# The last projection of a hybrid decoder block as seven half-size products for each pair of token tiles

## The chip, the core and the metric

The kernel runs on one core of a Trainium2 chip. The metric is the time of one execution on the device, in microseconds. The core has five engines that run side by side, each with its own queue of instructions, and meet by semaphores: TensorE (PE in the profile; its weight loads are PEld), VectorE (DVE), ScalarE (ACT), GpSimd (POOL) and SyncE (SP). SP mostly issues DMA transfers; POOL and ACT issue some too. TensorE writes its products to PSUM, eight banks of 128 x 512 float32. Everything else works in SBUF, 128 partitions wide.

## The reference

`x` holds 1024 tokens of 1024 channels. They are normalised and projected, and run through two token mixers (a dilated attention and a gated delta rule), whose outputs `o_a` and `o_b` are gated. The change touches only what comes after:

```python
y_a = (o_a * silu(dsa_z)) @ w_up_a          # 512 -> 1024
y_b = (o_b * silu(gdn_z)) @ w_up_b
merged = sigmoid(gate_a) * y_a + sigmoid(gate_b) * y_b
x = x + merged @ w_out                      # 1024 -> 1024
return rmsnorm(x, final_norm_w)
```

## The kernel before

**Precision.** Float32 products are made of float16 halves. Each operand is held as a high half (a cast, on ScalarE) and a low half (what the cast lost, one `scalar_tensor_tensor` on VectorE, line 76 by way of `STT`). `mm3_steps` (lines 169 to 179) makes three matmuls for each tile of 128 inner channels: high by high, high by low, low by high.

**Order.** TensorE's order is written out by hand: matmuls run in the order in which the program issues them. For the other engines a scheduler orders the instructions when the program is built, by priority (earlier in the program goes first, `tc.high_priority()` ahead of that) and by when it reckons them to be ready. On the chip each engine then runs its list strictly in order. `in_turn` (line 147) keeps an instruction behind the last matmul issued so far in that order, without a semaphore.

**The feed.** `Feed` (line 198) holds the projections as units of 28 or 32 steps, three matmuls of 512 columns each step, and loads and splits the next unit's weights while one runs. `feed.later(n, fn)` calls `fn` after n more steps. Many units are already made as seven products in place of eight (`seven_products`, line 347): their two-by-two blocks are added and subtracted beforehand, so that seven block products give all four blocks of the result.

**The last units.** Units `gate` 0 to 7 give the tanh of the merge gates, spilled to DRAM (`gsp`). Units `up` 0 to 3 (lines 1453 to 1483) each take two tiles (`dt`) of 128 channels. For each half of the tokens (`hf`, 512) they make the product of branch a in a bank `S` and that of branch b in a bank `mm`. VectorE multiplies each by its gate tile (`sig`, reloaded from DRAM), adds the two to `m` in float32, and ScalarE and VectorE split `m` into `m16`, two resident tiles of 1024 x 1024 float16 in the room of the input `h`. In the same units the output weights are loaded by POOL in eight pieces and split into `wo16`, one 128x1024 cast and one 128x1024 low half each.

**The last product.** Lines 1658 to 1687 go through eight token tiles of 128. For each half of the output columns, 8 channel tiles by 3 matmuls accumulate in a bank `mm`; VectorE adds the bank to `x`, ScalarE squares and sums it. Then come the root, the reciprocal, the scaling by `final_norm_w` and the store. The last tile cuts its second half in 384 and 128 columns, so that less is left after the last matmul. Tiles for gates, x and squares come from one ring of eight (`ring`, line 1640).

Of the kernel before, what the change touches and what calls it, by code (L numbers as in the profile page):

```python
# [10 lines left out]
F32 = mybir.dt.float32  # L11
F16 = mybir.dt.float16
# [8 lines left out]
KT = 8  # L21
# [43 lines left out]
PG_LAG = 20  # L65
PAIR_TICKS = 4
# [4 lines left out]
def hybrid_block(ctx: ExitStack, tc: tile.TileContext, A):  # L71
# [1338 lines left out]
    late, m16, wo16 = [], [], []  # L1410
# [17 lines left out]
    def z_now(br, ct, hf, p, rest):  # L1428
        ts = slice(hf * 512, hf * 512 + 512)
        gate = late[0].tile([128, 512], F32, name="zs", tag="zs", bufs=ZS)  # L1430
        z_silu(gate, p, rest)
        oa = late[0].tile([128, 512], F32, name="oa", tag="oa", bufs=2)
        nc.sync.dma_start(out=oa, in_=oa_d[ct, :, ts])
        STT(gate, gate, H_SCALE, oa, ALU.mult, ALU.mult)
        if (br, ct) not in osp:
            osp[br, ct] = late[1].tile([128, 2, S], F16, name=f"os{br}{ct}")
        n = osp[br, ct]
        SC.copy(n[:, 0, ts], gate)
        TT(n[:, 1, ts], gate, n[:, 0, ts], ALU.subtract)
# [12 lines left out]

    def up_unit(u):
        def gen(w):
            wh, wl = w
            for c in range(2):
                dt = 2 * u + c
                cs = slice(c * 128, c * 128 + 128)
                if c == 0:
                    us = slice(u * 256, u * 256 + 256)  # L1460
                    for n in range(2):
                        with tc.high_priority():
                            st = load_w(A["w_out"][u], n)
                        feed.later(14 + 8 * n, lambda st=st, n=n: (w_hi(st, wo16[0][:, :, us], n), w_lo(st, wo16[0][:, :, us], wo16[1][:, :, us], n)))
                for hf in range(2):
                    ts = slice(hf * 512, hf * 512 + 512)
                    for bi, br in enumerate("ab"):
                        p = bank("S", 2) if bi == 0 else bank("mm", 3)
                        for i, _ in enumerate(mm3_steps(
# [3 lines left out]
                            if i == 3:  # L1473
                                STT(sig[br, dt][:, ts], sig[br, dt][:, ts], 1.0, p, ALU.add, ALU.mult)
                            if i == 3 and bi:
                                m = sig["a", dt][:, ts]
                                TT(m, m, sig["b", dt][:, ts], ALU.add)
                                sc = 0.5 * P_SCALE * H_SCALE
                                SC.activation(m16[0][:, dt, ts], m, AF.Copy, scale=sc)
                                STT(m16[1][:, dt, ts], m, sc, m16[0][:, dt, ts], ALU.mult, ALU.subtract)  # L1480
# [156 lines left out]
    NR = 8  # L1637
    turn = [0]

    def ring(name):  # L1640
        turn[0] += 1
        if turn[0] % 2:
            return kp.tile([128, 16, 64], F32, name=name, tag="kT", bufs=4).rearrange("p a b -> p (a b)")
        return fp2.tile([128, S], F32, name=name, tag="sg2", bufs=4)

    for dt in range(8):
        for br in "ab":
            if len(sig) == NR:
                feed.until(("gate", 7))
            sig[br, dt] = ring(f"sg{br}{dt}")  # L1650
            nc.sync.dma_start(out=sig[br, dt], in_=gsp[br, dt])
    m16.extend(base.tile([128, KT, S], F16, name=f"m{n}", tag=f"h_{n}") for n in ("hi", "lo"))
    wo16.extend(fp2.tile([128, KT, D], F16, name=f"wo{n}") for n in range(2))

    feed.until(("up", 3))
    fw = fp2.tile([128, D], F32, name="fw")
    nc.sync.dma_start(out=fw, in_=A["fnw"])
    for t in range(8):
        tk = slice(t * 128, t * 128 + 128)
        xr = ring("xr")  # L1660
        nc.sync.dma_start(out=xr, in_=A["x"][tk])
        ss = fp2.tile([128, 4], F32, name="ss", tag="ss", bufs=2)
        junk = ring("junk")
        y = ring("y") if t == 7 else xr
        edges = (0, 512, 896, 1024) if t == 7 else (0, 512, 1024)
        for c, (c0, c1) in enumerate(zip(edges, edges[1:])):
            cs = slice(c0, c1)
            p = bank("mm", 3)[:, :c1 - c0]
            mm3(p, (lambda k: m16[0][:, k, tk], lambda k: m16[1][:, k, tk]),
                (lambda k: wo16[0][:, k, cs], lambda k: wo16[1][:, k, cs]))  # L1670
            STT(xr[:, cs], p, P_SCALE, xr[:, cs], ALU.mult, ALU.add)
            SC.activation(junk[:, :c1 - c0], xr[:, cs], AF.Square, accum_out=ss[:, min(c, 1):min(c, 1) + 1])  # L1672
            if c:
                TT(ss[:, 0:1], ss[:, 0:1], ss[:, 1:2], ALU.add)
            if t == 7:
                TT(y[:, cs], xr[:, cs], fw[:, cs], ALU.mult)
        r = ss[:, 3:4]
        SC.activation(ss[:, 2:3], ss[:, 0:1], AF.Sqrt, bias=epsc, scale=1.0 / D)
        V.reciprocal(r, ss[:, 2:3])
        if t < 7:  # L1680
            STT(xr, xr, r, fw, ALU.mult, ALU.mult)
            nc.sync.dma_start(out=A["out"][tk], in_=xr)
        else:
            V.tensor_scalar(y[:, :640], y[:, :640], r, None, op0=ALU.mult)
            nc.sync.dma_start(out=A["out"][tk, :640], in_=y[:, :640])
            SC.activation(y[:, 640:], y[:, 640:], AF.Copy, scale=r)
            nc.scalar.dma_start(out=A["out"][tk, 640:], in_=y[:, 640:])
# [58 lines left out]
def _layout(x, norm_w, w_in, conv_w, a_log, dt_bias, gdn_norm_w, w_up_a, w_up_b, w_out, final_norm_w):  # L1746
# [28 lines left out]
        "w_out": c(unit(np.asarray(w_out)[0])),  # L1775
# [17 lines left out]
```

## Time and profile before

| | |
|---|---|
| median of 3 runs | 1108.44 us (1108.34 to 1109.62) |
| the profiled execution | 1110.44 us, of which the profile's span is 1108.7 us |
| TensorE, VectorE, ScalarE, POOL busy | 96%, 75%, 50%, 5% of the span |
| up units | 936.6 to 1019.5 us of the span |
| last product | 1019.5 to 1102.4 us |
| after the last matmul | 1102.4 to 1108.7 us |

A row of a group reads: line, engine, operation, output<-input, shapes, count, then busy us and mean ns of one, then the idle time of the engine just before these instructions and what ended it. A row of the timeline reads: start, duration, engine, line, operation. A row of the stages gives for each engine its busy time and number of instructions in that stretch, then the granted TensorE clock, the DMA share and GB/s.

### The profile page before, as it was taken

The page shows a single profiled execution, that of the slowest core. Times are in us where ns is not written, and L with a number is a line of the kernel's source. Part 1 is how long each engine was busy: PE and PEld are TensorE (multiplying, and loading weights), DVE is VectorE, ACT ScalarE, POOL GpSimd, SP SyncE. Part 2 cuts the span into 40 slices and gives each one's busy share as a digit, 9 for nine tenths or more (in the row PEclk, how much of TensorE's full clock was granted, in tenths as well). Part 3 has the DMA queues.
Part 4 walks back from the last instruction along what each step waited for, and adds up shares of the span by engine and source line. Part 5 has one row for each costly group of instructions (what it writes and reads, how often), then busy time and mean ns, then how long its engine had stood idle before and what let it go on. Part 6 is the DMA issues. An engine that isn't in the chain of part 4 may idle for free. (4 is left out here: it accounts for less than half of the span.)

```text
span 1108.7 us, 23803 instructions
## 1 busy us (share of the span) xinstructions
PE 1063.1 (96%) x9486; PEld 645.3 (58%) x9486; DVE 829.7 (75%) x1918; ACT 556.1 (50%) x1239; POOL 57.3 (5%) x103
## 2 busy tenths in 40 slices
PE   6999999999999999989999999899999999999997
PEld 5894585775956755756555545445545554444443
DVE  5798997969879679969955997963488777775223
ACT  6455766667666566456635533343454344331211
POOL 1200000000000000000000000000000000110000
PEclk9999999999999999999999999999999999999999
DMA  8135521623516333631235267794785414762221
GB/s 285 62 90 139 135 63 68 168 78 87 140 63 172 88 101 87 156 99 58 69 105 174 69 167 187 219 261 143 232 257 163 144 64 149 250 210 71 76 95 57
DMA packets 102926, 146.88 MB, mean 132 GB/s; under 512 B 31120, under 2 KB 68496, under 8 KB 101920
## 3 DMA queue, kind: packets, MB, share of 16 engines
q1 hardware_dynamic: 79856, 91.49, 28.7%
q0 software_dynamic: 12128, 44.11, 12.7%
q10 hardware_dynamic: 10832, 9.77, 2.7%
q8 instruction: 74, 1.21, 0.5%
q14 instruction: 36, 0.29, 0.1%
HBM read 89.56 MB, written 36.90 MB: 114 GB/s over the span
## 5 line engine op out<-in xcount | busy, mean ns | idle before, releaser
L177 PE MATMUL ps_mm<-h_hi,wlo 128*128 128x512 f16 (+1 forms) x552 | 208.0, 377 | 2.6 <-DVE wlo L76 2.6
L176 PE MATMUL ps_mm<-h_lo,whi 128*128 128x512 f16 (+1 forms) x492 | 185.5, 377 | 2.6 <-issue 1.8
L175 PE MATMUL ps_mm<-h_hi,whi 128*128 128x512 f16 (+1 forms) x492 | 185.7, 377 | 0.0
L177 PEld LDWEIGHTS <-wlo 128*128 128x128 f16 x788 | 77.2, 98 | 92.7 <-issue 3.9
L176 PEld LDWEIGHTS <-whi 128*128 128x128 f16 x848 | 83.1, 98 | 70.9 <-issue 4.8
L175 PEld LDWEIGHTS <-whi 128*128 128x128 f16 x848 | 83.1, 98 | 70.4 <-issue 0.8
L175 PE MATMUL ps_mm<-whi,h_hi 128*128 128x256 f16 x384 | 105.1, 274 | 0.0
L177 PE MATMUL ps_mm<-whi,h_lo 128*128 128x256 f16 x384 | 104.7, 273 | 0.0
L176 PE MATMUL ps_mm<-wlo,h_hi 128*128 128x256 f16 x384 | 104.7, 273 | 0.0
L774 ACT ACTIVATE sm<-sm,osb 128x128 f32<-128x128 f32 (+1 forms) x160 | 69.7, 436 | 56.1 <-DVE osb L770 52.8
L79 DVE TENSOR_TENSOR tl<-ps_G,th 128x256 f16<-128x256 f32 (+1 forms) x96 | 52.1, 542 | 18.6 <-ACT th L789 18.5
L79 DVE TENSOR_TENSOR rt<-rx,tabs 128x512 f32<-128x512 f32 x96 | 64.6, 688 | 1.4 <-ACT rx L580 0.4
L76 DVE SCALAR_TENSOR_TENSOR wlo<-wstage,whi 128x1024 f16<-128x1024 f32 x50 | 61.0, 1222 | 5.7 <-ACT whi L158 5.4
L770 DVE CUSTOM_DVE_ANT_0 sm<-ps_S,amask 128x128 f32<-128x128 f32 (+1 forms) x192 | 59.4, 348 | 7.6 <-PE ps_S L763 7.6
L76 DVE SCALAR_TENSOR_TENSOR ca<-xc,cw,ca 128x512 f32<-128x512 f32 x72 | 53.9, 749 | 9.7 <-ACT ca L997 8.8
L76 DVE SCALAR_TENSOR_TENSOR whi<-wstage,whi 128x512 f16<-128x512 f32 x60 | 40.7, 688 | 20.7 <-ACT whi L322 20.0
L158 ACT ACTIVATE whi<-wstage 128x1024 f16<-128x1024 f32 x49 | 51.6, 1053 | 6.2 <-DMA wstage<-in_w_up 5.2
L784 PE MATMUL ps_G<-cons,sm 128*128 128x128 f32 x280 | 48.3, 276 | 4.8 <-ACT sm L774 2.9
L175 PE MATMUL ps_mm<-wo,mhi 128*128 128x512 f16 (+2 forms) x136 | 49.5, 366 | 0.0
L176 PE MATMUL ps_mm<-wo,mhi 128*128 128x512 f16 (+2 forms) x136 | 49.5, 366 | 0.0
L177 PE MATMUL ps_mm<-wo,mlo 128*128 128x512 f16 (+2 forms) x136 | 49.4, 366 | 0.0
L784 PEld LDWEIGHTS ps_G<-cons,sm 128*128 128x128 f32 x280 | 35.6, 141 | 21.7 <-ACT sm L774 6.5
(335 smaller groups left out, 2538.3 us busy)
## 6 DMA issues: line engine op xcount, KB each, us to landing
wstage<-in_w POOLq DMA_DIRECT2D x68, 512.0 KB, 4.7
og<-osb ACTq DMA_DIRECT2D x32, 132.0 KB, 2.3
og<-og SPq DMA_DIRECT2D x32, 132.0 KB, 2.3
gspa<-gst SPq DMA_DIRECT2D x16, 256.0 KB, 2.2
sga<-gspa SPq DMA_DIRECT2D x8, 512.0 KB, 5.3
wstage<-in_w_up POOLq DMA_DIRECT2D x8, 512.0 KB, 5.2
sgb<-gspb SPq DMA_DIRECT2D x8, 512.0 KB, 5.5
wstage<-in_w_out POOLq DMA_DIRECT2D x8, 512.0 KB, 4.0
```

Source lines behind the costliest of these rows:

```text
L76: (eng or V).scalar_tensor_tensor(out, in0, scalar, in1, op0=op0, op1=op1)
L79: (eng or V).tensor_tensor(out, in0, in1, op)
L158: in_turn(SC.activation(hi[:, 4 * c:4 * c + 4], st, AF.Copy, scale=W_SCALE))
L175: PE.matmul(out, lhsT=wh(k), rhs=mh(k), start=first and i == 0, stop=False, skip_group_check=True)
L176: PE.matmul(out, lhsT=wh(k), rhs=ml(k), start=False, stop=False, skip_group_check=True)
L177: last_pe[0] = PE.matmul(out, lhsT=wl(k), rhs=mh(k), start=False, stop=last and i == len(ks) - 1, skip_group_check=True).ins.name
L770: V.tensor_tensor_reduce(P[:, u, :128 * nk], psc[:, u * 256:u * 256 + 128 * nk], mask, -cexp, -NEG, ALU.add, ALU.min, accum_out=osb[:, 256 ...
L774: SC.activation(P[:, u, :128 * nk], P[:, u, :128 * nk], AF.Exp, bias=osb[:, 256 + hd:257 + hd], scale=-1.0, accum_out=osb[:, 260 + hd:261 ...
L784: PE.transpose(pt[:, c:c + 128], P[:, u, i * 128:i * 128 + 128], ident)
```

## The change

The last product becomes seven products for each pair of token tiles. Take a pair of token tiles (even, odd) as two block rows, the two halves of the 1024 inner channels as x and y, and the weights as four blocks b11, b12, b21, b22 (inner half, output half). With x0, y0 of the even and x1, y1 of the odd tile, the seven left factors are x0, x0+x1, x0+x1+y1, y0, x1+y1, y1 and x0+y0+x1+y1. The right ones are b11, b22-b12, a sum of three blocks, b21, b11-b12, a sum of four, and b22. Each product has four channel tiles in place of eight, with 512 columns.

- `split_wo` loads one group of four 128x512 blocks (one channel tile of each half, by SP into a ring `sgc` of two tiles), makes four sums in float32 and seven splits. It runs four times, from step 14 after the pool is opened (in the last gate unit) and from step 24 of up units 0, 1 and 2. All 14 halves stay resident.
- `m_parts` makes the sums of m and their splits, 256 tokens (two pairs) at a time, for each tile: for the first half of the tokens in the up units at high priority, for the second half in the first pair of the last product.
- The gates are loaded two tiles ahead (`load_sig`); branch b's ring has two tiles.
- In the last product three banks are used for each pair (`G`, `G`, `mm` and `mm` three times in turn). Two bank-to-bank copies on ScalarE carry partial sums. Product 1's bank is subtracted from both halves of the odd tile by VectorE before product 2 is copied into it.
- The last pair ends with the even tile, whose product 6 is cut in 384 and 128 columns.

```diff
+        put(0, b11)
+        in_turn(V.tensor_tensor(b11, b11, b12, ALU.subtract))
+        put(4, b11)
+        TT(b12, b22, b12, ALU.subtract)
+        put(1, b12)
+        put(6, b22)
+        STT(b22, b22, -1.0, b11, ALU.mult, ALU.subtract)
+        put(2, b22)
+        put(3, b21)
+        STT(b21, b22, -1.0, b21, ALU.mult, ALU.subtract)
+        put(5, b21)
+        if kk < 3:
+            load_wo(kk + 1)
...
+        def put(n, y):
+            hi, lo = [m7[hf][n][:, l, kk].rearrange("p (a i) -> p a i", a=2) for l in range(2)]
+            in_turn(SC.activation(hi, y, AF.Copy, scale=M_SCALE))
+            STT(lo, y, M_SCALE, hi, ALU.mult, ALU.subtract)
+
+        if k < 4:
+            put(0, x0)
+            TT(x0, x0, x1, ALU.add)
+            put(1, x0)
+            return
...
+        TT(x0, x0, y1, ALU.add)
+        put(2, x0)
+        put(3, y0)
+        TT(x1, x1, y1, ALU.add)
+        put(4, x1)
+        put(5, y1)
+        TT(y0, y0, x0, ALU.add)
+        put(6, y0)
...
-                if c == 0:
-                    us = slice(u * 256, u * 256 + 256)
-                    for n in range(2):
-                        with tc.high_priority():
-                            st = load_w(A["w_out"][u], n)
-                        feed.later(14 + 8 * n, lambda st=st, n=n: (w_hi(st, wo16[0][:, :, us], n), w_lo(st, wo16[0][:, :, us], wo16[1][:, :, us], n)))
+                load_sig(dt + SIG_AHEAD)
+                if c == 0 and u < 3:
+                    feed.later(WO_LAG, lambda: split_wo(u + 1))
...
-                                STT(sig[br, dt][:, ts], sig[br, dt][:, ts], 1.0, p, ALU.add, ALU.mult)
+                                with tc.high_priority():
+                                    STT(sig[br, dt][:, ts], sig[br, dt][:, ts], 1.0, p, ALU.add, ALU.mult)
...
-                                SC.activation(m16[0][:, dt, ts], m, AF.Copy, scale=sc)
-                                STT(m16[1][:, dt, ts], m, sc, m16[0][:, dt, ts], ALU.mult, ALU.subtract)
+                                if hf == 0:
+                                    with tc.high_priority():
+                                        m_parts(dt, 0)
...
-            mm3(p, (lambda k: m16[0][:, k, tk], lambda k: m16[1][:, k, tk]),
-                (lambda k: wo16[0][:, k, cs], lambda k: wo16[1][:, k, cs]))
...
+        with tc.high_priority():
+            product(0, x, True)
+            SC.copy(y, x)
+            product(1, q, True)
+        if pair == 0:
+            for k in range(4):
+                m_parts(k, 1)
+        with tc.high_priority():
+            for j in (1, 0):
+                rows_[1].add(q, half(j), -1.0)
+            product(2, x)
+            SC.copy(q, x)
+            product(3, y)
+            rows_[0].add(y, half(0))
+            rows_[0].square(half(0))
+        if pair == 0:
+            for k in range(4, 8):
+                m_parts(k, 1)
+        with tc.high_priority():
+            product(4, q)
+            rows_[1].add(q, half(1), -1.0)
+            rows_[1].square(half(1))
+            product(5, x)
+            rows_[1].add(x, half(0), -1.0)
+            rows_[1].square(half(0))
+            rows_[1].finish()
+            if pair < 3:
+                product(6, q)
+                rows_[0].add(q, half(1))
+                rows_[0].square(half(1))
+                rows_[0].finish()
```

`add` is the VectorE addition of a bank to a half of a token tile of x, `square` the sum of squares on ScalarE, `finish` the root, the reciprocal, the scaling of 128x1024 and the store.

More of the change, by code (lines that the diff above doesn't have):

```diff
@@ L1652, in hybrid_block @@
[L1652 to L1653 removed]
+    late.append(fp2)
+    load_wo(0)
+    feed.later(WO_FIRST, lambda: split_wo(0))
+    for dt in range(SIG_AHEAD):
+        load_sig(dt)
+    room = [base.tile([128, KT, S], F16, name=f"m{n}", tag=f"h_{n}").rearrange("p k s -> p (k s)") for n in ("hi", "lo")]
+    m7.append([room[n // 4][:, 2048 * (n % 4):2048 * (n % 4) + 2048].rearrange("p (l k i) -> p l k i", l=2, i=256)
+               for n in range(7)])
```

148 lines of the change are left out of this document (104 added, 44 removed).

## The prediction

> **What bounds the kernel now.** I read the page's head first, then busy time stage by stage, then the matmuls one by one at the seams of the last product.
>
> ```profile
> span 1108.7 us, 23803 instructions
> ...
> PE 1063.1 (96%) x9486; PEld 645.3 (58%) x9486; DVE 829.7 (75%) x1918; ACT 556.1 (50%) x1239; POOL 57.3 (5%) x103
> ```
>
> The page has TensorE busy for 96% of the span; the stages say whether that holds where the change is made.
>
> ```profile
> core 0: us, PE busy (x) PEld busy (x) DVE busy (x) ACT busy (x) POOL busy (x), PEclk, DMA share, GB/s
> 917.20:935.40 18.20, 17.40 (x120) 7.96 (x118) 17.25 (x33) 9.90 (x16) 1.59 (x3) 1.00 0.26 89
> 936.60:1019.50 82.90, 82.90 (x386) 37.60 (x385) 56.36 (x75) 24.09 (x30) 6.36 (x12) 1.00 0.57 194
> 1019.50:1102.40 82.90, 82.90 (x409) 38.85 (x407) 25.47 (x42) 15.29 (x41) 0.00 (x0) 1.00 0.21 76
> 1102.40:1108.70 6.30, 0.20 (x4) 0.02 (x1) 1.57 (x7) 1.47 (x6) 0.00 (x0) 0.87 0.22 83
> ```
>
> The rows are: most of the last gate unit, the four up units, the last product, and the tail after the last matmul. In the up units and the last product TensorE has no gap at all, at a granted clock of 1.00. So matmuls taken out there shorten the span one for one, as long as nothing else becomes late. VectorE is busy for 56.4 of 82.9 us in the up units and 25.5 of 82.9 in the last product: room in the second, little in the first.
>
> ```profile
> 1019.49 0.38 PE L175 MATMUL ps_mm<-wo,mhi 128*128 128x512 f16 x1
> ...
> 1092.01 0.38 PE L175 MATMUL ps_mm<-wo,mhi 128*128 128x512 f16 x1
> ...
> 1096.98 0.38 PE L177 MATMUL ps_mm<-wo,mlo 128*128 128x512 f16 x1
> ...
> 1102.38 0.22 PE L177 MATMUL ps_mm<-wo,mlo 128*128 128x128 f16 x1
> ```
>
> A matmul lasts 0.38 us but the next starts earlier: 1092.01 to 1096.98 are 24 matmuls of one half tile, 23 steps, so 4.97/23 = 0.216 us each. The last product runs from 1019.49 to 1102.4 plus a short drain.
>
> **Matmuls removed.** Before, eight token tiles by two halves by eight channel tiles by three matmuls make 384 matmuls of 512 columns (the last tile's second half is cut in 384 and 128, the same columns). 384 x 0.216 = 82.9, which is the stage. After, four pairs by seven products by four channel tiles by three make 336, with 512 columns again and again one product cut in two. That removes 48 x 0.216 = **10.4 us** of TensorE's time. The other terms ask how much of it is handed back.
>
> **Work added on VectorE before the last product.** Per stage the diff gives: of m, for the first half of the tokens, channel tiles 0 to 3 have two parts and one addition each, tiles 4 to 7 five parts and three additions; 28 parts and 16 additions of 128x256. A part is one ScalarE cast (high half) and one VectorE instruction (low half), so VectorE gets 44 instructions. Of the output weights, four groups of seven parts and four sums make 28 ScalarE casts and 44 VectorE instructions of 128x512. Gone are the 16 m casts and their low halves and the eight weight splits:
>
> ```profile
> L76 DVE SCALAR_TENSOR_TENSOR mlo<-sga,mhi 128x512 f16<-128x512 f32 x16 | 11.1, 692 | 5.6 <-ACT mhi L1479 4.9
> L76 DVE SCALAR_TENSOR_TENSOR xr<-ps_mm,xr 128x512 f32<-128x512 f32 x15 | 10.4, 692 | 44.1 <-PE ps_mm L177 44.1
> L1479 ACT ACTIVATE mhi<-sga 128x512 f16<-128x512 f32 x16 | 10.1, 631 | 47.6 <-DVE sga L79 47.6
> L76 DVE SCALAR_TENSOR_TENSOR wo<-wstage,wo 128x1024 f16<-128x1024 f32 x8 | 9.8, 1224 | 5.7 <-ACT wo L158 5.7
> L76 DVE SCALAR_TENSOR_TENSOR xr<-xr,ss,fw 128x1024 f32<-128x1024 f32 x7 | 9.0, 1285 | 0.2
> L158 ACT ACTIVATE wo<-wstage 128x1024 f16<-128x1024 f32 x8 | 8.4, 1052 | 7.1 <-DMA wstage<-in_w_out 7.0
> ```
>
> What one instruction holds of VectorE lies between two prices, both in the next rows, from the timeline and the groups:
>
> ```profile
> 913.21 4.91 DVE L79 TENSOR_TENSOR ob<-ob,fac 128x512 f32<-128x512 f32 x8
> ...
> 932.84 2.35 DVE L76 SCALAR_TENSOR_TENSOR wlo<-wstage,whi 128x1024 f16<-128x1024 f32 x2
> ```
> ```profile
> L79 DVE TENSOR_TENSOR og<-og,f 128x256 f32<-128x256 f32 x32 | 12.4, 421 | 0.3
> L322 ACT ACTIVATE whi<-wstage 128x512 f16<-128x512 f32 x60 | 37.0, 628 | 14.4 <-DVE wstage L321 8.8 <-PE ps_mm L176 2.9 <-PE ps_mm L177 2.3
> L359 ACT COPY ps_mm<-ps_mm 128x512 f32<-128x512 f32 x30 | 17.2, 573 | 20.2 <-PE ps_mm L177 16.8 <-DMA gspb<-gst 2.0 <-ACT osb L816 0.8
> L1008 ACT ACTIVATE qT<-ca 128x256 f32<-128x256 f32 x8 | 2.9, 411 | 9.9 <-DVE ca L76 9.9
> ```
>
> Eight instructions of 0.69 us in a row take 4.91, so a 128x512 costs (4.91 - 0.69)/7 = 0.60 when the next one is ready; a 128x1024 costs 2.35 - 1.22 = 1.13; 32 of 128x256 took 12.4, 0.39 each. At these prices the up units lose 16 x 0.60 + 8 x 1.13 = 18.6 and gain 44 x 0.60 + 44 x 0.39 = 43.6: 56.4 + 25.0 = **81.4 of 82.9 us**. At full durations they lose 20.9 and gain 44 x 0.69 + 44 x 0.42 = 48.8: 84.3, more than the stage. The trace's rows in a run are the better likeness, since the new work comes in dense bursts, so I take 81.4 and keep 84.3 as the bound. ScalarE goes from 24.1 to 24.1 - 10.1 - 8.4 + 28 x 0.41 + 28 x 0.63 = 34.7 of 82.9 and isn't the bound.
>
> The Trainium skill speaks for the dearer price: in "VectorE: DVE Perf Modes", section Terms, a drain follows every operation and the next cannot issue until the pipe is empty. By that rule the 84.3 would hold; the eight starts 0.60 apart at 0.69 us each disagree, and the row decides.
>
> The second half of the tokens costs the same 44 instructions, 17.2 us, inside the first pair of the last product, and has until the third pair. A pair lasts 84 x 0.216 = 18.1 us; its own VectorE work is six additions at 0.60, two scalings at 1.285 and about 0.6 of small ones, 6.8 us. The third pair reads sums of channel tile 7 from its third product on, at 1019.5 + 36.3 + 5.2 = 1061. From 936.6 to there VectorE has 124.4 us for 81.4 + 17.2 + 13.6 = 112.2: slack 12.2 (7.0 at full durations). What is queued behind a late instruction is everything else on VectorE, the additions that free PSUM banks among them.
>
> **First seam.** Product 0 needs all four weight groups; the last one is due at step 24 of the third up unit, 40 steps of 0.65 us, 26 us, ahead of the end, and has 11 instructions (6.6 us) under evictions that go first. The parts of channel tile 7 come from a sum that stands 4 to 5 us before the up units end, and are read 5.2 + 1.9 us after it. So the cover is about 8 us; each us of VectorE backlog above it is a us of TensorE. With 98% demand I allow **1.5 us** for this and for the seam at the third pair; bounds 0 and 14 (worked out below).
>
> **Handovers inside a pair.** The new copies from bank to bank (row L359, 0.57 us) and each addition (0.69) lie under one product of 12 x 0.216 = 2.6 us before the bank is written again. I cost them at nothing; without the cover it is 0.6 to 1.4 us a handover, and what then waits is the next product.
>
> **Loads.** The weight loads move from POOL's queue to SP's, where the sigmoid tiles, x and the outputs are queued in order too.
>
> ```profile
> sgb<-gspb SPq DMA_DIRECT2D x8, 512.0 KB, 5.5
> wstage<-in_w_out POOLq DMA_DIRECT2D x8, 512.0 KB, 4.0
> xr<-in_x SPq DMA_DIRECT2D x8, 512.0 KB, 3.4
> out<-xr SPq DMA_DIRECT2D x7, 512.0 KB, 2.6
> ```
> ```profile
> 934.32 1.75 SPq L1651 DMA_DIRECT2D sgb<-gspb  x4
> ```
>
> Four loads went out at 934.3, when the memory came free; now two of weights and two of sgb will, as many bytes. The ring of sgb has two tiles: one is freed when the sum of its second half is made, some 2 us into the next channel tile, lands 5.5 later, and is needed 10.4 + 5.2 after that tile's start: cover 8 us, and two more banks after that. In the last product x(t+4) waits for an output to leave: an order of 2.6 + 3.4 us within 18. Nothing, again; a gone cover costs one product, 2.6 us.
>
> **The tail.** Before, the last tile's 384-column piece was 1.3 us ahead of its last matmul and VectorE was free. Now it is 12 short matmuls ahead, 0.7 us, and the scaling of the other tile of the pair (1.285 us) becomes ready at about the same moment.
>
> ```profile
> 1101.29 0.56 DVE L76 SCALAR_TENSOR_TENSOR xr<-ps_mm,xr 128x384 f32<-128x384 f32 x1 [2.48 <-PE ps_mm L177]
> ...
> 1102.67 0.28 DVE L76 SCALAR_TENSOR_TENSOR xr<-ps_mm,xr 128x128 f32<-128x128 f32 x1
> ...
> 1104.20 0.61 ACT L1686 ACTIVATE y<-y,ss 128x384 f32<-128x384 f32 x1 [0.23 <-DVE ss L1679]
> ...
> 1104.78 0.33 SPq L1685 DMA_DIRECT2D out<-y  x1
> ```
>
> The chain from 1102.67 on keeps all its steps. Its first one is late by 0.6 us (the 384 piece still on VectorE) if the scaling comes after it, and by some 2.0 if before. I take **+1.7**, between 0.5 and 2.5.
>
> **The sum.** -10.4 + 1.7 + 1.5 = -7.2 us. The profiled execution took 1110.4 (span 1108.7 and 1.7 around it), 2.0 above the median of the three runs; it would become 1103.2 with a span near 1101.5, and the median 1108.4 - 7.2 = **1101.2**. The forecast's own range, with the tail's bounds and 0 to 4 us of stalls, is 1098.5 to 1104.
>
> **Rivals.**
> (a) *VectorE's backlog reaches TensorE in part*: 5 to 10 us of stall, at the first products of pair 0 or at pair 2. For it: 98% demand. Time 1108.4 - 10.4 + 1.7 + 5 to 10 = 1104.7 to 1109.7; by the middle, about 1107, a small gain or none. Within 0.2% (2.2 us, what a measurement here can tell from no change) is 1106.2 to 1110.7, its upper part.
> (b) *Slower: each low half waits for its high half.* The new work has 84 ScalarE-to-VectorE handoffs up to 1061 (28 of weights, 56 of m).
>
> ```profile
> DVE wo L76 <- ACT wo L158: 5.7, 6, 2.0
> DVE mlo L76 <- ACT mhi L1479: 4.9, 7, 0.7
> ```
>
> The 16 low halves of m waited 4.9 us in all, 0.31 each. If the order written for VectorE leaves each new one that wait, 84 x 0.31 = 26 us, 14 beyond the slack: 1108.4 - 10.4 + 1.7 + 14 = **1114**. It decides from (12.2 + 8.7)/84 = 0.25 us per handoff on. Against it: those waits were made while VectorE had nothing else, and in the last gate unit (first stage row) it reached 17.25 of 18.20 us on work of this kind with 0.8 us of TensorE idle. "TensorE: Matmul & The Clock Gate" of the Trainium skill, section "What's actually happening", adds that an idle window of some 3.4 us halves the clock until work has filled the next one, by which such a stall would cost an estimated 1.7 us more; no gap in these stages is long enough to show it.
> (c) *Nothing is handed back*: the scheduler hides the tail and every stall, 1108.4 - 10.4 + 0.5 = 1098.5 or a little under.
>
> **How the numbers follow.** Forecast 0.62, (a) 0.19, (b) 0.12, (c) 0.07. Faster by over 0.2%: 0.62 + 0.07 + two thirds of (a) = 0.81; within 0.2%: the rest of (a) and a little of (b), 0.07; slower 0.12. The range takes (a) to its middle and most of (c): 1098.2 to 1107.5.
>
> **What would show it.** Right: 48 x 512 columns fewer in the last stage, no TensorE gap over a us from the up units to the last matmul, VectorE over 95% busy in the up units, a tail of 7 to 9 us after the last matmul. Wrong: a TensorE gap just before product 0, 1 or 2 of the first pair that ends with a low half of wo or m (the first seam), or in the third pair (second half of the tokens), or low halves of m and wo that idle VectorE for 0.25 us each (b). An sgb eviction that waits for its load would show the rings too short, which I cost at nothing.

## The result and the profile after

On one chip the kernel before took 1109.03 us (median of 4, 1108.34 to 1111.58) and the changed kernel **1100.66 us** (median of 4, 1098.58 to 1101.08). The ratio is 0.9917, with a 95% interval of 0.9896 to 0.9938. The profiled execution of the changed kernel took 1101.08 us, of which 1099.3 are its span.

The head of the page of the changed kernel:

```profile
span 1099.3 us, 23863 instructions
...
PE 1053.7 (96%) x9426; PEld 640.4 (58%) x9426; DVE 867.3 (79%) x2034; ACT 577.6 (53%) x1307; POOL 53.1 (5%) x95
```

TensorE has 60 matmuls fewer: the 48 removed, and 12 because the half tile that is cut in two pieces is now 12 matmuls made twice where it was 24. VectorE has 116 instructions more and 37.6 us more of busy time. TensorE's share is still 96%, so it is still the bound, of a shorter span. The stages of the changed kernel show where: four rows for the four up units, one for the last product, one for what follows its last matmul (columns as in the stages of before).

```profile
935.50:956.20 20.70, 20.70 (x97) 9.40 (x96) 13.98 (x23) 8.22 (x13) 0.53 (x1) 1.00 0.81 292
956.20:977.00 20.80, 20.80 (x98) 9.46 (x97) 20.80 (x37) 9.32 (x16) 1.59 (x3) 1.00 0.74 245
977.00:997.70 20.70, 20.70 (x98) 9.35 (x97) 20.70 (x39) 9.97 (x19) 0.00 (x0) 1.00 0.54 187
997.70:1018.40 20.70, 20.70 (x98) 9.39 (x97) 20.17 (x43) 6.47 (x16) 0.00 (x0) 1.00 0.33 101
1018.40:1091.90 73.50, 72.68 (x349) 33.52 (x347) 42.91 (x93) 28.01 (x76) 0.00 (x0) 1.00 0.23 79
1091.90:1099.30 7.40, 0.18 (x4) 0.00 (x1) 2.39 (x8) 1.31 (x5) 0.00 (x0) 0.68 0.36 142
```

VectorE is busy for every microsecond of the second and third up unit, and TensorE still has no gap in any of the four. The last product takes 73.5 us where it took 82.9, and all but 0.82 of it is matmuls. Two places are read from the timeline of the changed kernel: the seams at which the last product needs new parts, and the end.

```profile
935.50 0.38 PE L178 MATMUL ps_S<-osa,whi 128*128 128x512 f16 x1
...
943.51 0.69 DVE L79 SCALAR_TENSOR_TENSOR sgb<-sgb,ps_mm 128x512 f32<-128x512 f32 x1 [3.92 <-PE ps_S L180]
...
1016.85 0.42 DVE L79 SCALAR_TENSOR_TENSOR mhi<-sga,mhi 128x256 f16<-128x256 f32 x1
...
1018.38 0.38 PE L178 MATMUL ps_G<-wo0h,mhi 128*128 128x512 f16 x1
...
1025.51 0.38 PE L178 MATMUL ps_G<-wo2h,mhi 128*128 128x512 f16 x1
...
1029.99 1.76 DVE L79 SCALAR_TENSOR_TENSOR mb<-sga,mb 128x256 f16<-128x256 f32 x5
...
1046.21 0.43 DVE L79 SCALAR_TENSOR_TENSOR mb<-sga,mb 128x256 f16<-128x256 f32 x1 [0.30 <-ACT mb L1514]
...
1054.64 0.38 PE L178 MATMUL ps_G<-wo0h,mb 128*128 128x512 f16 x1
...
1090.65 0.54 DVE L79 SCALAR_TENSOR_TENSOR xr<-ps_mm,xr 128x384 f32<-128x384 f32 x1
1091.11 1.27 DVE L79 SCALAR_TENSOR_TENSOR xr<-xr,ss,fw 128x1024 f32<-128x1024 f32 x1
1091.25 0.22 PE L178 MATMUL ps_mm<-wo6h,mb 128*128 128x128 f16 x1 [0.82 <-DVE xr L79]
...
1091.86 0.22 PE L180 MATMUL ps_mm<-wo6h,mb 128*128 128x128 f16 x1
...
1092.84 0.28 DVE L79 SCALAR_TENSOR_TENSOR xr<-ps_mm,xr 128x128 f32<-128x128 f32 x1
...
1094.95 0.33 SPq L1835 DMA_DIRECT2D out<-y  x1
```

Product 2 of a pair is the first that reads parts of channel tiles 4 to 7. At the first seam the parts of tile 7 that products 2 and 3 read are both ready at 1017.27; product 2 starts at 1018.38 + 2 x 2.6 = 1023.6 and comes to tile 7, its fourth, at 1025.51, 8.2 us after they are ready. At the second, the last part for the second half of the tokens is ready at 1046.64, 13 us before product 2 of the third pair starts (1054.64 + 5.2 = 1059.8). The only gap of TensorE is the 0.82 us near the end. There the 128-column piece of the last half tile waits for VectorE, which is still reading the 384-column piece from the same bank; before, the two pieces had banks of their own. After the last matmul VectorE is still at the scaling of the odd tile, and has one product with `fw` besides, ahead of the last addition.

Three stretches, cut at the first up matmul, the first matmul of the last product and the start of the last matmul, give the balance of the profiled executions (936.61, 1019.49 and 1102.38 of a span of 1108.7 before):

| us | up units | last product | after the last matmul's start | sum |
|---|---|---|---|---|
| before | 82.88 | 82.89 | 6.32 | 172.09 |
| after | 82.88 | 73.48 | 7.44 | 163.80 |

So the change is worth **-8.29 us** from the first up matmul on: -10.39 of matmuls (82.89 to 72.50, the last product without a gap, which a run below shows), +0.98 for the gap and the matmuls around it, +1.12 after the last matmul's start.

### The profile page after: what moved, and what is told of

It is laid out like the page before. It is cut to its first block, busy times and chain, and to the rows that moved or that the text cites. A ratio compares the mean times of both kernels' runs of the same rounds, so it can differ in the third digit from the quotient of the medians.

```text
span 1099.3 us, 23863 instructions
## 1 busy us (share of the span) xinstructions
PE 1053.7 (96%) x9426; PEld 640.4 (58%) x9426; DVE 867.3 (79%) x2034; ACT 577.6 (53%) x1307; POOL 53.1 (5%) x95
## 4 chain that ended last, share of the span: by engine, by line
PE 55%; DVE 29%; ACT 7%; DMA 5%; issue 3%; SPq 1%; POOL 0%; ACTq 0%; DVEq 0%; POOLq 0%
PE ps_mm L178 13%; PE ps_mm L180 13%; PE ps_mm L179 13%; DVE rt L82 3%; DVE wlo L79 3%; DVE ca L79 2%; DVE sm L773 2%; ACT sm L777 2%; DVE tl L82 2%; DVE ro L82 2%; DVE pcAl L82 1%; PE ps_S L179 1%; PE ps_S L178 1%; PE ps_S L180 1%; DVE pcBl L82 1%
## 5 line engine op out<-in xcount | busy, mean ns | idle before, releaser
L179 PEld LDWEIGHTS <-h_hi 128*128 128x128 f16 x384 | 45.8, 119 | 1.7
L178 PEld LDWEIGHTS <-h_hi 128*128 128x128 f16 x384 | 45.7, 119 | 1.6
L178 PE MATMUL ps_mm<-h_hi,wlo 128*128 128x512 f16 x120 | 45.6, 380 | 0.8 <-DVE zs L79 0.5
```

The source lines that it names most:

```text
L178: PE.matmul(out, lhsT=wh(k), rhs=mh(k), start=first and i == 0, stop=False, skip_group_check=True)
L179: PE.matmul(out, lhsT=wh(k), rhs=ml(k), start=False, stop=False, skip_group_check=True)
```

## The experiments

All runs are the changed kernel, unedited or with an edit, but for one that edits the kernel before. The medians stand beside the kernel before on the same chip. Sums are those of the table above, made in the same way from each run's trace.

### Does the changed kernel give anything back?

The changed kernel once more, unedited:

> The changed kernel as it is, beside the others on the same chip. Theory: 48 matmuls of 512 columns less (10.4 us), 0.8 us given back in a TensorE gap before the last 128 columns and 1.1 us more between the last matmul and the end: about 8.4 us faster than before, ratio 0.992. Rival: the start of the profiled executions (first matmul 1.0 us earlier after than before) is part of the gain; then about 9.4 us.

1100.9 us against 1109.62, ratio 0.9922 (0.9901 to 0.9943); sum 163.76. A second repetition, in a later comparison on another chip:

> The changed kernel as it is, beside e10_tail on the same chip. Counted from the first matmul of the up units: 163.8 us as before, with 0.8 us of gap before the last piece and 7.4 us after the last matmul.

1100.63 against 1110.04, ratio 0.9923 (0.9904 to 0.9942); sum 163.82. In the three traces of the changed kernel the sum from the first up matmul repeats within 0.06 us, while executions of one kernel spread over some 5 us (1099.02 to 1104.22 in the second of these). The spread comes in ahead of the seam: in all thirteen traces of this document it is 66.4 to 66.5 us from TensorE's 8001st matmul to the first up matmul, but the 8001st itself lies anywhere from 865.8 to 871.5. So an edit is priced by its sum, and its median only says whether it agrees.

The gains of the medians are 8.4, 8.7 and 9.4 us, and their intervals are too wide to tell these from the 8.29 of the traces. The rival of the first repetition, that up to 1 us of gain comes ahead of the seam, isn't borne out: these 66.4 us are the same in both kernels, and what differs lies earlier, ahead of the first work of the change.

Next, the kernel before with the same 48 matmuls left out of it, and none of the new work. It leaves the last of the eight channel tiles out of the last product:

```diff
             mm3(p, (lambda k: m16[0][:, k, tk], lambda k: m16[1][:, k, tk]),
-                (lambda k: wo16[0][:, k, cs], lambda k: wo16[1][:, k, cs]))
+                (lambda k: wo16[0][:, k, cs], lambda k: wo16[1][:, k, cs]), ks=range(7))
```

> The kernel before with channel tile 7 of 8 left out of the last product (its result lacks that part): 48 matmuls of 512 columns less and none of the added work. Theory: 10.4 us faster than before (ratio 0.9907), so the changed kernel gives back 1.9 us of it. Rival (VectorE's 44 + 44 added instructions cost TensorE time that the trace hides): the difference to the changed kernel is 4 us or more.

Its timeline, first up matmul, first and last matmul of the last product:

```profile
937.96 0.38 PE L175 MATMUL ps_S<-osa,whi 128*128 128x512 f16 x1
...
1020.84 0.38 PE L175 MATMUL ps_mm<-wo,mhi 128*128 128x512 f16 x1
...
1093.36 0.22 PE L177 MATMUL ps_mm<-wo,mlo 128*128 128x128 f16 x1
```

The last product takes 72.52 us; with a span of 1099.8 the sum is 161.84, 10.25 below before. The matmuls are worth what 48 x 0.216 says, and the changed kernel gives back 163.80 - 161.84 = 1.96 us of it, all of it at the end; the rival's 4 us or more did not come. The median, 1101.67 (ratio 0.9930, 0.9906 to 0.9954), can't tell it from the changed kernel: its first up matmul was at 937.96, 2.5 us later than that of the changed kernel, in a program that is that of the kernel before up to there.

### What makes up the end

A bank of its own for each of the two pieces of the last half tile:

```diff
+            if pair == 3:
+                rows_[0].add(q, half(1))
             product(5, x)
...
             for cs in (slice(0, 384), slice(384, 512)):
-                product(6, q, cs=cs)
-                last.add(q[:, cs], half(1, cs))
+                p = bank("S", 2)
+                product(6, p, True, cs=cs)
+                last.add(p[:, cs], half(1, cs))
```

> In the last pair product 6 gets two fresh banks, one for each of its pieces, and the even tile takes what stood in the bank before it by one more VectorE addition under product 5. Theory: the 0.82 us gap of TensorE before the 128 columns goes, and the end comes 0.6 to 0.9 us earlier than in the changed kernel. Rival (VectorE sets the tail: the scaling of the odd tile runs 1091.1 to 1092.4 whatever TensorE does): the end moves by less than 0.3 us.

The end of its timeline (its first up matmul is at 934.00):

```profile
1089.38 0.22 PE L180 MATMUL ps_S<-wo6h,mb 128*128 128x128 f16 x1
...
1089.63 1.28 DVE L79 SCALAR_TENSOR_TENSOR xr<-xr,ss,fw 128x1024 f32<-128x1024 f32 x1
1090.89 0.55 DVE L82 TENSOR_TENSOR y<-xr,fw 128x384 f32<-128x384 f32 x1
1091.36 0.28 DVE L79 SCALAR_TENSOR_TENSOR xr<-ps_S,xr 128x128 f32<-128x128 f32 x1
```

The gap is gone and the last product takes 72.50 us, but the sum is 163.80, to the hundredth that of the changed kernel (median 1100.35, ratio 0.9922, 0.9900 to 0.9944). The last matmul starts 1 us sooner, and the last addition 1.98 after it in place of 0.98: it is behind 1.28 + 0.55 us on VectorE either way. The gap of TensorE and VectorE's queue lie on top of each other; only the queue counts.

So, besides, the odd tile's scaling is taken apart: its product with `fw` is made half by half as the sums come, and what is left for the end is one scaling by a number for each row.

```diff
+            if pair == 3:
+                o7 = fp2.tile([128, S], F32, name="y7", tag="sga", bufs=4)
+                TT(o7[:, 512:], rows_[1].x[:, 512:], fw[:, 512:], ALU.mult)
...
-            rows_[1].finish()
+            if pair == 3:
+                TT(o7[:, :512], rows_[1].x[:, :512], fw[:, :512], ALU.mult)
+                V.tensor_scalar(o7, o7, rows_[1].norm(), None, op0=ALU.mult)
+                nc.sync.dma_start(out=A["out"][rows_[1].tk], in_=o7)
+            else:
+                rows_[1].finish()
```

> As own_banks, and the odd tile of the last pair is multiplied by the final weights half by half as its sums come, so that only a multiplication by the reciprocal (a tensor_scalar of 128x1024) is left for the moment when the last pieces arrive. Theory: both causes of the longer tail go: gap 0.8 and 0.7 on VectorE: 1.2 to 1.8 us earlier than the changed kernel. Rival (the two stores that end together, 512 KB and 512 KB, set the end): less than 0.5 us beyond own_banks.

```profile
1091.32 0.22 PE L180 MATMUL ps_S<-wo6h,mb 128*128 128x128 f16 x1
...
1091.56 0.75 DVE L1825 TENSOR_SCALAR y<-y,ss 128x1024 f32<-128x1024 f32 x1
1092.21 0.55 DVE L82 TENSOR_TENSOR y<-xr,fw 128x384 f32<-128x384 f32 x1
1092.75 0.28 DVE L79 SCALAR_TENSOR_TENSOR xr<-ps_S,xr 128x128 f32<-128x128 f32 x1
```

The scaling takes 0.75 in place of 1.28 and the last addition comes 1.43 after the last matmul in place of 1.98. The sum is 163.25, 0.55 less: the 0.53 of the shorter scaling and no more, since the scaling still stands ahead of the last addition in VectorE's list. The expectation was too high. (Median 1099.65, ratio 0.9916, 0.9894 to 0.9937.)

The other way is to have the odd tile's scaling ready sooner: banks as in the first of these, and in the last pair the even tile's first half (product 3) is made after product 5, so that a whole product lies between the odd tile's last sum and the end.

```diff
-            product(3, y)
-            rows_[0].add(y, half(0))
-            rows_[0].square(half(0))
+            def third():
+                product(3, y)
+                rows_[0].add(y, half(0))
+                rows_[0].square(half(0))
+
+            if pair < 3:
+                third()
...
             rows_[1].finish()
+            if pair == 3:
+                third()
```

> As own_banks, and in the last pair product 3 comes after product 5, so that the odd tile is done 2.6 us earlier and its scaling no longer stands in VectorE's queue ahead of the last piece. Nothing then covers the copy from bank to bank between products 2 and 4. Theory: TensorE waits 0.6 to 1.0 us there (copy 0.57 and the way to it), and the tail is 1.4 to 1.9 us shorter than in own_banks; together 0.5 to 1.3 us earlier than the changed kernel, counted from the first matmul of the up units. Rival (the two stores set the end): no gain.

VectorE's and TensorE's rows of its timeline:

```profile
1079.62 0.38 PE L178 MATMUL ps_mm<-wo4h,mb 128*128 128x512 f16 x1 [0.66 <-ACT ps_mm L1804]
...
1089.96 0.22 PE L180 MATMUL ps_S<-wo6h,mb 128*128 128x128 f16 x1
...
1090.85 0.28 DVE L79 SCALAR_TENSOR_TENSOR xr<-ps_S,xr 128x128 f32<-128x128 f32 x1
```

The scaling leaves the end (it runs from 1087.26 to 1088.54), and the stretch after the last matmul's start falls from 8.42 to 7.44 us. It stays longer than the 6.32 of before, since the addition of product 3 and its product with `fw` now stand late in VectorE's list: the last addition starts 0.89 us after the last matmul. And now product 4 follows product 2 at once, and ScalarE's copy from bank to bank between them, which had a product of another bank over it, stops TensorE for 0.66 us; with the matmuls around it this costs 0.82 (73.32 - 72.50). The sum is 163.64, a gain of 0.16, less than the expected 0.5 (median 1099.44, ratio 0.9911, 0.9893 to 0.9930). It is the run that takes the cover from a handover of the change, and the prediction's price for that, 0.6 to 1.4, is confirmed in its lower part.

All of it together: product 3 is split, two channel tiles between products 2 and 4 as a cover for the copy, two after product 5 as a cover for the scaling, with the separate banks and the scaling taken apart.

```diff
-            product(3, y)
-            rows_[0].add(y, half(0))
-            rows_[0].square(half(0))
...
+            if pair < 3:
+                third()
+            else:
+                product(3, y, ks=range(2))
...
+                third(range(2, 4))
```

> The changed kernel with four edits to the last pair: product 6 in two fresh banks; the odd tile multiplied by the final weights as its halves come; half of product 3 left between products 2 and 4, where it covers the copy; its other half after product 5, so that the odd tile is done before the last pieces. Theory: no gap (0.8 us less), and no wait of the last piece on VectorE (0.7 us less): counted from the first matmul of the up units 82.9 + 72.5 + 6.8 = 162.2 us, 1.6 us less than the changed kernel. Rival (the 0.4 us at the very end and the queue on VectorE stay): 163.2 or more.

```profile
1087.25 0.75 DVE L1831 TENSOR_SCALAR y<-y,ss 128x1024 f32<-128x1024 f32 x1
...
1087.67 0.22 PE L180 MATMUL ps_S<-wo6h,mb 128*128 128x128 f16 x1
1087.92 0.75 DVE L79 SCALAR_TENSOR_TENSOR xr<-ps_S,xr 128x384 f32<-128x384 f32 x2
...
1091.14 0.33 SPq L1853 DMA_DIRECT2D out<-y  x1
```

There is no gap, and still the sum is 163.21: 0.6 below the changed kernel, not the whole 1.96. That is the rival of the expectation, 163.2 or more. The scaling still stands ahead of both last additions on VectorE, and ScalarE's last square, at 1089.41, waits for VectorE once more. The store leaves 3.47 us after the start of the last matmul, where it was 1104.78 - 1102.38 = 2.40 in the kernel before: 1.07 of the 1.51 us by which this end is longer than that one (7.83 against 6.32). Its first up matmul lies at 932.29 and its span is 1095.5. Its median is 1098.58 (ratio 0.9910, 0.9890 to 0.9931), the lowest of all, but intervals that overlap so far can't tell it from the changed kernel: by its trace it is the better one, by its time it isn't shown.

The other 0.44 lie behind the store, and the unedited changed kernel has them as well. SP's waits over the last 20 us name a place, first for the kernel before, then for the changed kernel:

```profile
SPq L1789 <- PEq L1789: 0.7, 2, 0.5
```
```profile
SPq L1939 <- PEq L1939: 1.1, 2, 0.9
```

From the start of the last store to the end of the span it is 1108.7 - 1104.78 = 3.92 us before and 1099.3 - 1094.95 = 4.35 after. SP's wait for the store is the same, 2.1 us; the wait of the program's last line for TensorE's queue is 0.4 longer. It is so in every variant of the changed kernel whose end was read (4.3 to 4.4 us with the scaling early, the third product late and all together), also where the odd tile's store had left long before, while the kernel before with seven channel tiles has 0.6 there as the kernel before has 0.7. What in the new program makes it so is **open**; no run tells.

### How much room VectorE has

The forecast rests on VectorE's slack. It was measured by filling it: behind the last eviction of each half tile in the up units, and ahead of its sum in the program, VectorE makes an addition of 128x512 into a tile that nobody reads, 16 in all, by the prediction's 0.60 some 9.6 us.

```diff
                             if i == 3:
+                                for _ in range(bi):
+                                    d = wst.tile([128, 512], F32, name="dum", tag="x7", bufs=1)
+                                    TT(d, cons[:, :512], cons[:, :512], ALU.add)
```

> The changed kernel with 16 more VectorE additions of 128x512 in the up units (into a scratch tile that nobody reads), 16 x 0.60 = 9.6 us, while its VectorE is already busy for 20.7 of 20.7 us in up units 1 and 2. Theory: work that nobody waits for moves behind the evictions, which have priority, and into the 7 us that VectorE idles in the first up unit and the 3.6 after the up units; the last one of the up units' results was 5 to 6 us early. So TensorE waits under 1 us. Rival (VectorE at 100% is the bound of the up units): each us added is a us of TensorE, +9.6 us.

The sum is 164.28, 0.48 more than without (median 1099.99, ratio 0.9918, 0.9900 to 0.9937). Its stages: third up unit, and the first pair of the last product.

```profile
977.90:998.60 20.70, 20.70 (x98) 9.39 (x97) 20.70 (x39) 8.58 (x16) 0.00 (x0) 1.00 0.47 164
1019.30:1037.80 18.50, 18.23 (x85) 8.21 (x84) 17.91 (x45) 10.91 (x33) 0.00 (x0) 1.00 0.17 56
```

The up units are still without a gap. VectorE is busy there for 80.70 us in place of 75.65, mostly in the first of them, where it had idled, and in the first pair for 17.9 of 18.5 us in place of 14.8; a copy by ScalarE there holds TensorE for 0.27. So of 9.6 us more, 9.1 disappear. With 48 additions, 28.9 us (three for each half tile in place of one, the first of them behind branch a's eviction):

> As vector_plus_10 with 48 such additions, 28.9 us. Theory: some 7 + 6 us of it are hidden up to the first pair, and the rest makes TensorE wait there, before product 0 to 2 of the first pair: 10 to 18 us. Rival (bound all along): +29 us in gaps inside the up units. Other rival (VectorE's load is hidden wherever it stands): under 3 us.

```profile
1007.57 0.61 PE L180 MATMUL ps_S<-osa,wlo 128*128 128x512 f16 x1 [8.99 <-DVE wlo L79]
...
1010.10 0.49 PE L180 MATMUL ps_S<-osa,wlo 128*128 128x512 f16 x1
...
1010.64 0.38 PE L179 MATMUL ps_S<-osa,whi 128*128 128x512 f16 x1
...
1037.24 0.39 PE L178 MATMUL ps_G<-wo2h,mhi 128*128 128x512 f16 x1 [0.75 <-ACT mhi L1514]
```
```profile
998.58:1007.57 8.99, 0.00 (x0) 0.00 (x1) 8.27 (x18) 2.90 (x7) 0.00 (x0) 0.77 0.29 98
1007.57:1009.57 2.00, 2.00 (x5) 0.73 (x6) 2.00 (x3) 0.00 (x0) 0.00 (x0) 0.50 0.00 0
```

1113.76 us, ratio 1.0036 (1.0023 to 1.0049); the sum is 176.31, 12.5 more, so 16.4 of the 28.9 are hidden. The size is near the forecast's, but the place isn't: TensorE stops for 8.99 us inside the up units, for the low half of the *up weights* of the last unit, which stands in VectorE's list behind the additions and the sums of m. The stage row shows VectorE at work for 8.27 of these 8.99 us. Where the expectation looked, before the products of the first pair, there is little: product 2 waits twice for parts of m, 0.75 and 0.48 us, and the last product is 1.65 us longer than in the changed kernel. No split of the output weights is late.

The gap shows a second thing. In the 2 us after it the granted clock is 0.50, and from 1007.57 to 1010.64 there are 8 steps of TensorE in 3.07 us; at 0.216 they would take 1.73. The long gap costs 1.3 us more than itself. "TensorE: Matmul & The Clock Gate" of the Trainium skill, section "What's actually happening", has a clock that falls to one half after an idle window of about 3.4 us and comes back after a busy one as long. The trace agrees on the half; it came back after some 2.7 us here, and the 1.3 us stand against the 1.7 that the prediction had worked out as an estimate from that page of the Trainium skill.

If it is the place in the list that matters, the split of the up weights ahead of the additions should bring the time back:

```diff
-            w_hi(self.st[c], self.blocks[0], c)
-            w_lo(self.st[c], *self.blocks, c)
+            with tc.high_priority() if self.hot else nullcontext():
+                w_hi(self.st[c], self.blocks[0], c)
+                w_lo(self.st[c], *self.blocks, c)
...
-        feed.add(("up", u), Normal(A["w_up"][u]), gen)
+        feed.add(("up", u), Normal(A["w_up"][u], True), gen)
```

> As vector_plus_29, whose largest stall, 9.0 us, came when up unit 3 waited for the low halves of its own weights; here the splits of the up units' weights have high priority. Theory (those splits are the first work of VectorE that TensorE runs out of): the 9 us gap goes; since the 28.9 us of additions are still there, part of it comes back at the first pair: 2 to 7 us in place of 12.5. Rival (VectorE has no room left at all): the total stays within 2 us of the 176.3 us of vector_plus_29, and the gap only moves.

A single run took 1120.28 us, with a sum of 183.20, 19.4 above the changed kernel: worse than the 12.5. The longest of TensorE's waits from 930 us on (us in total, times, longest), and a stage row of the first pair:

```profile
PE ps_G L178 <- ACT mhi L1516: 5.7, 2, 5.1
PE ps_G L178 <- ACT ps_mm L1801: 3.0, 1, 3.0
```
```profile
1031.28:1046.10 14.82, 7.24 (x17) 1.92 (x16) 14.82 (x33) 5.95 (x17) 0.00 (x0) 0.50 0.32 108
```

The gap of 9 us goes, as the theory said, and the up units take 86.15 us in place of 93.71. But the first pair pays far more than the 2 to 7 us: the last product takes 89.59 in place of 75.13, and its waits are those of rival (a). Neither the theory's total nor the rival's, within 2 us of 176.3, came out. The stage row shows a part of the reason: the waits follow one another so closely that the granted clock is 0.50 for 14.8 us, from before the end of a wait of 2.96 us on. What the run does show is that the place of the stall is a matter of the order written for VectorE, and that the backlog is paid somewhere.

Last, the priority that the change gives to the evictions and the parts of m in the up units is taken away:

```diff
                             if i == 3:
-                                with tc.high_priority():
-                                    STT(sig[br, dt][:, ts], sig[br, dt][:, ts], 1.0, p, ALU.add, ALU.mult)
+                                STT(sig[br, dt][:, ts], sig[br, dt][:, ts], 1.0, p, ALU.add, ALU.mult)
...
                                 if hf == 0:
-                                    with tc.high_priority():
-                                        m_parts(dt, 0)
+                                    m_parts(dt, 0)
```

> The changed kernel without the high priority of the evictions and of the sums of m in the up units (the kernel before had none there either). Theory: behind a block of weight splits (11 instructions, 6.6 us) an eviction comes up to 6.6 us late; branch a has two banks of 5.2 us each, so TensorE waits up to 1.5 us per block in the up units, and the sums of tile 7 come later at the first pair: 2 to 8 us in all. Rival (the scheduler's order by readiness is enough): under 0.5 us.

```profile
962.82 0.38 PE L178 MATMUL ps_S<-osa,whi 128*128 128x512 f16 x1 [0.70 <-DVE sga L79]
```

The sum is 164.80, 1.0 more, with one gap of 0.70 in the second up unit, for an eviction that frees a bank (median 1101.95, ratio 0.9935, 0.9919 to 0.9951). The priority helps, by less than was expected, and its loss doesn't undo the change: VectorE's room is there in either order.

## Why the prediction was right, point by point

The forecast of 1101.2 was made of -10.4 + 1.7 + 1.5 = -7.2 us; the traces give -8.29 and the medians of one chip -8.4. That it lies within 0.5 us of the measured 1100.66 is in part luck: the change is worth 1.1 us more than forecast (the stalls were 1.5 too dear, the tail 0.4 too cheap), and beside it the kernel before took 1109.03, 0.6 more than the 1108.44 from which the forecast started.

**Matmuls removed, -10.4: right.** 82.89 - 72.50 = 10.39 between the kernel before and the run with banks of their own, and the kernel before with seven channel tiles has the same 72.5.

**Stalls at the seams, +1.5: the term that was mis-sized; it measured 0.** No gap of TensorE in the up units or the first three pairs. The failing step is the price of VectorE's work: 81.4 of 82.9 us was forecast, 84.3 as the bound, and the four stages give 13.98 + 20.80 + 20.70 + 20.17 = **75.65**. For a 128x256 the prediction took 0.39, the mean of 32 that didn't all follow one another closely; the row at 1029.99 has five in 1.76 us, (1.76 - 0.42)/4 = 0.335. Over 44 instructions that is 2.4 us. (ScalarE came out near its forecast of 34.7: 8.22 + 9.32 + 9.97 + 6.47 = 33.98.) The other 3.4 are in the 56.4 of before that the sum started from: there, instructions that stand alone count with all of their 0.69, and in a full list they count with 0.60. Of these, 46 of 128x512 and 6 of 128x1024 stay, which the prediction carried over at 56.4 - 18.6 = 37.8; at the dense prices they are 46 x 0.60 + 6 x 1.13 = 34.4. With the new 44 x 0.60, and 43 x 0.335 for the parts of m that fall into the stage, that makes 75.2, near the 75.65. This second part is worked out so, not measured apart.

The section "The TRN2 errata — SBUF-src ops pay a fixed extra latency per instruction" of "VectorE: DVE Perf Modes" in the Trainium skill has a table with 58 + elements cycles at 0.96 GHz, which is 0.59 us for 512 and 0.33 for 256: the spacing of starts that these rows show, 0.60 and 0.335, though that page of the Trainium skill takes it for a duration and finds it too short for one. Estimated by it, the 44 parts of 128x256 would have been priced right, and the forecast of VectorE's load 2.4 us nearer.

**Slack at the second seam, 12.2 us: near.** The parts were 13 us early, and 9.6 us of added work cost 0.5. **Cover at the first seam, 8 us: right**, it is 8.2, and nothing in the unedited kernel eats it up.

**Rival (b), 0.31 us for each low half: refuted.** The groups of the changed kernel from the last gate unit on (line, engine, operation, count, then busy us, mean ns, and idle before):

```profile
L79 DVE SCALAR_TENSOR_TENSOR mb<-sga,mb 128x256 f16<-128x256 f32 x28 | 10.8, 418 | 0.3 <-ACT mb L1514 0.3
L79 DVE SCALAR_TENSOR_TENSOR mhi<-sga,mhi 128x256 f16<-128x256 f32 x16 | 6.5, 418 | 0.0
...
L79 DVE SCALAR_TENSOR_TENSOR mlo<-sga,mlo 128x256 f16<-128x256 f32 x12 | 4.9, 419 | 0.5 <-ACT mlo L1514 0.5
...
L79 DVE SCALAR_TENSOR_TENSOR wo0l<-wos,wo0h 128x512 f16<-128x512 f32 x4 | 2.7, 685 | 0.0
```

The 56 low halves of m waited 0.8 us in all, 0.014 each, and the row of the weights stands for seven like it with 0.0. VectorE had other work while ScalarE made each cast, as the prediction held against this rival. **Rival (a)** needed a backlog; it takes between 10 and 29 us of added work to make one, and it then comes first where the prediction hadn't looked, at the weights of the up units, or in the first pair, by the order of the list. **Rival (c)**, nothing handed back, is out by 1.96 us at the end.

**Handovers at 0: right**; with the cover taken from one of them it was 0.82, of which 0.66 are a wait.

**Loads at 0: right for the time, less so in the ring.** In the first up unit VectorE stood idle for 3.92 us before the first eviction of branch b at 943.51. The row names a product of branch a, but branch b's own product had ended at 940.85, and the gate tile `sgb`, whose load went out at 934.07, took 9.3 us to land, until 943.4. In the second repetition of the same kernel the row names the load:

```profile
943.26 0.69 DVE L79 SCALAR_TENSOR_TENSOR sgb<-sgb,ps_mm 128x512 f32<-128x512 f32 x1 [4.20 <-DMA sgb<-gspb]
```

So the sign that the prediction gave, an eviction that waits for its load, did appear. It had reckoned with 5.5 us from issue to landing; the three loads of `sgb` around the first up unit took 7.5 to 12.5. Two weight loads now go out ahead of them; whether these are the cause wasn't tried. TensorE had the other banks and lost nothing.

**The tail, +1.7: 2.10 (0.98 + 1.12), and only part of the mechanism.** VectorE's queue was foreseen, with the scaling ahead of the last addition: that addition starts 0.98 us after the last matmul in place of 0.29, 0.69 more. Not foreseen were the shared bank (0.98; without it the queue takes the same 0.98, as the banks' run shows) and the 0.43 of the program's end. Queue and bank together are 1.67. With banks of their own it is the queue alone, with the last addition 1.98 us after the last matmul in place of 0.29, 1.69 more: the forecast's 1.7 was the right size for the queue, and the shared bank hid behind it.

**The signs.** No gap over 1 us and 7.44 us of tail: as said. VectorE over 95% busy in the up units: only in three of the four, 91% over all of them.

**Two slips in the working** touch neither the forecast nor the terms. 1108.4 - 10.4 + 2.5 + 4 is 1104.5, not 1104. And of rival (a)'s 1104.7 to 1109.7 some 30%, not two thirds, lies below 1106.2, where the prediction lets a gain begin.

## What to carry to other kernels

Price an engine that is to be filled by the distance between starts in a dense row, not by the durations of instructions that stand alone: the second can say over 100% where 91% comes out. Fewer matmuls on a TensorE without gaps pay in full, as here, as long as every new operand is ready with some us to spare, and then it is the last few us, where no next product covers anything, that decide what is given back. An engine that is 100% busy need not be late: look at when its results are read, and fill its room with work that nobody reads to see how much of it there is and what is late first.

## What was not expected of the hardware

- Executions of one kernel differ by 5 us and more (the kernel before: 1105.77 to 1112.46 in eleven), but in three traces of the changed kernel the time from the first up matmul to the end is the same within 0.06 us. In the variants of the changed kernel that matmul lay anywhere from 932.3 to 936.4. What varies is ahead of TensorE's 8001st matmul, most of it (423.2 to 426.3 us) between the 3001st and the 7001st; its cause was not looked into.
- VectorE was busy for 41.5 us without a pause beside a TensorE without a gap.
- In the run with the weight splits first, the granted clock was 0.50 after waits of 1.36 and 2.96 us with 0.6 us of matmuls between them, so no single wait as long as 3 us was needed.
- From the last store to the end of the program it takes 0.4 us longer in all variants of the changed kernel, in a wait of SP for TensorE's queue.
